# Weights fetched through ScalarE's queue, the keys' sums in another pool, and the second layer's cached keys turned during the first layer's projections

## The chip, the core and the metric

The kernel runs on one NeuronCore of a Trainium2 chip. The metric is device time in microseconds of one execution of the program; times are compared as medians of several executions. In the profile, PE is TensorE (matrix multiplication), PEld its weight loads, ACT is ScalarE, DVE is VectorE, POOL is GpSimd, and SP is the engine that issues most DMAs. An engine's DMA-issuing instructions carry a q behind the engine's name (SPq, ACTq).

## What is computed

A two-layer encoder step on 2048 prompt frames and 64 sample frames, model width 1024, 16 heads of 64, all in fp32. Layer A is attention within a band of chunks with softmax, layer B a stick-breaking attention over all earlier frames:

```python
def reference(x_prompt, x_sample, cache_a_k, cache_a_v, cache_b_k, cache_b_v, norm_a, w_in_a, ...):
    qp, kp, vp, gp = a_project(xp, norm_a[i], w_in_a[i])       # RMSNorm, then one 1024 x 4096 projection
    op = chunk_band_prompt(qp, kp, vp, rel_bias_a[i])          # own chunk and 8 before it, softmax
    o_s = band_attend(qs, cache_a ++ ks, cache_a ++ vs, ...)
    xp = xp + gated_out(op, gp, w_out_a[i])                    # (o * silu(gate)) @ w_out
    kb_p, vb_p = shared_kv(xp, norm_kv, w_kv)                  # keys and values of layer B
    qp, gp = b_project(xp, norm_b[j], w_in_b[j])
    op = sb_prompt(qp, kb_p, vb_p)                             # w = exp(log_sigmoid(z) + sum of later log_sigmoid(-z))
    o_s = sb_block(qs, cache_b ++ kb_s, cache_b ++ vb_s, ...)
    xp = xp + gated_out(op, gp, w_out_b[j])
    y_prompt = rms_norm(xp, norm_f)
```

The outputs are the normed streams and the new rows of both key/value caches. Layer B's cache has 2048 rows, so its keys have to be brought into the layout [channel, row] once: this is the work that the change moves.

## The kernel before

Every fp32 product is split: an operand x is held as a high part (rounded to the format fp32r) and a low part, and hi·hi + hi·lo + lo·hi are added up in PSUM. Nothing fits into SBUF at once, so queries, keys, values, gates and outputs go through DRAM scratch tensors (`lay[L]`), as high and low parts.

The program has four stretches, two for each layer:

1. **Projections** (`projections`): first the values (tiles `ps_v`), then 24 jobs (three kinds by 8 head pairs, tiles `ps_t`): load a weight block (`wraw`, by ACT's queue), scale and split it, multiply, split the result, store it. Half of some kinds is left for later (`DEFER`): keys in layer A, queries and gates in layer B. Beside each job `stages.pop(0)` runs a share of a list of other preparations: `stage_cache` (load cached keys `kr`, turn them on PE as four 128x128 transposes `ps_c`, split, store), `stage_bias`, `stage_diff` (differences of values, on POOL), `stage_w_out` (split layer B's output weights and store them as `wo`). Before the change layer A's list has 56 entries, of which the last 8 are layer B's cached keys (8 of 32), and layer B's list has 74, of which 24 are the other cached keys.
2. **Attention**: items of four score tiles each (`z`), their weighting, transposes (`wt`), the split on ACT and DVE (`ph`, `pl`) and the products with the values (`acc`). An object `Beat` writes one item's parts out in beats, and beside them runs the steps of a second list, `beat.beside`: first the jobs left for later (`late_job`, products `ps_j`, weights `lwh` and `lwl`), then the output weights into two 4 MB tiles (`w_out_steps`, tiles `big`), then the output projection (`out_tile`, products `ps_o`). `Beat.step` takes one step at a time; each entry of the list has loads that run `ahead`, products, and work `behind`. The load of the next entry is started at the first product of the entry before.

What sets the order: the tile scheduler orders the instructions of each engine, except that within the attention the instructions that go through the wrapped engines (`InOrder`; `act`, `dve`, `gps`, `pe`, and `sp` for queue loads) keep the order in which the program is written. Each queue issues its DMAs in order, and a DMA waits at the head of its queue until its semaphores allow it. The semaphores of DMAs are eight (DMAHW0 to 7, handed out over all queues): a DMA also waits until the one before it on its semaphore has landed.

Names that the prediction uses: `vt`, `kt`, `q` are values, keys and queries loaded for the attention; `lkn` (in `add_back`) is the sum of a late key block's high and low part, made on POOL for the output rows; `sg` is a gate tile, stored as `gate_a` at the end of a projection job; `og`, `xr` are loads of the output projection. Tiles of a later stretch lie in memory that tiles of an earlier stretch have left, and then wait for their last readers, stores among them. All instructions that go through the wrapped engines show line L90 of the kernel (the wrapper); loads by the attention's `Queue` show L134, its stores L127.

Of the kernel before, what the change touches and what calls it, by code (L numbers as in the profile page):

```python
# [21 lines left out]
NP = 2048  # L22
# [28 lines left out]
STEP = 2  # L51

# [48 lines left out]
def encoder_step(ctx: ExitStack, tc: tile.TileContext, a: dict, o: dict):  # L101
# [634 lines left out]
    def late_job(L, kind, w, c0, g, hp, x2, first, prompt, rows_pool):  # L736
        st = {}

        def load():
            if L not in KEPT:  # L740
                st["raw"] = opool.tile([P, NK, P], F32, name="lraw", tag="og", bufs=1)
                c = c0 + hp * P
                sp.dma_start(st["raw"], w[:, c : c + P].rearrange("(k p) c -> p k c", p=P))
            st["wh"] = opool.tile([P, NK, P], F32R, name="lwh", tag="oh", bufs=2)
            st["wl"] = opool.tile([P, NK, P], F32R, name="lwl", tag="ol", bufs=2)
            if L in KEPT:
                for i, part in enumerate((st["wh"], st["wl"])):
                    sp.dma_start(f32(part), f32(lay[L]["w"][kind, hp][i]))
# [56 lines left out]
    def w_out_steps(src, w):  # L805
# [3 lines left out]
        def parts(k):  # L809
            if k == 0:  # L810
                w.extend(big_pair())
            for i in range(2):
                sp.dma_start(f32(w[i][:, k]), f32(wod[k][:, i]))
# [86 lines left out]
    class Beat:  # L900
# [4 lines left out]
        def __init__(self, lag, hold, scores_first, blank):  # L905
# [5 lines left out]
            self.now, self.at, self.ready, self.started = None, 0, 0, False  # L911
# [12 lines left out]
        def step(self):  # L924


            if self.now is None:
                self.now, self.at = self.beside.pop(0), 0
                ahead = self.now[0]
                if ahead and not self.started:  # L930

                    ahead.pop(0)()
                    self.ready = self.clock + 9
                self.started = False
# [16 lines left out]
            if self.at == 0 and following:  # L951
                rest.append(following.pop(0))
                self.started = True
# [7 lines left out]
            if self.at > half or n == 1:  # L961
                m = -(-len(following) // (n - self.at + 1))
                rest += [following.pop(0) for _ in range(m)]
# [100 lines left out]
    staged += keys_b[:8]  # L1064
    staged_b = []
    for i, (t, half) in enumerate((t, half) for t in range(len(TOK)) for half in range(2)):
        staged_b += [partial(stage_diff, "new", t, half), *keys_b[8 + i : 9 + i]]
# [19 lines left out]
    with (  # L1087
# [11 lines left out]
        beat.beside = job_steps("a", jobs_a, x2, NP - CACHE_A, o["a_k_p"], lpool)  # L1099
# [164 lines left out]
    with (  # L1264
# [45 lines left out]
        beat.beside = job_steps("b", jobs_b, x2, 0, o["b_k_p"], lpool)  # L1310
# [238 lines left out]
```

## Time and profile before

| | |
|---|---|
| median of three runs | 3279.95 us (3270.53, 3279.95, 3283.12) |
| profiled execution | 3271.0 us, its span 3269.2 us |
| granted TensorE clock, mean of the span | 0.996 |
| busy: PE, DVE, ACT, POOL | 98%, 58%, 52%, 40% |
| layer A: values, jobs, attention | 0 to 213, 213 to 668, 668 to 1312 us |
| layer B: values, jobs, attention and end | 1312 to 1624, 1624 to 2014, 2014 to 3269 us |

The page of the profile gives busy times of the engines, the span in 40 slices, the DMA queues, the chain of work that ended last, and the costliest groups of instructions. Busy time of PE is a modelled one: matmuls overlap, so 98% doesn't say that PE runs at its peak, but idle time of PE is real. Beside the page the trace is asked for the busy time of each engine and the granted clock in chosen stretches, for who waited for whom, for the chain in order of time, and for the instructions of one engine in order of time.

### The profile page before, as it was taken

What the parts mean: (1) busy time and instruction counts of PE and PEld (TensorE: products, weight loads), DVE (VectorE), ACT (ScalarE), POOL (GpSimd) and SP (SyncE); (2) the same over time, 40 slices, a digit from 0 to 9 for tenths busy, and PEclk for the clock granted to TensorE, in tenths of its full rate; (3) what the DMA queues carried; (4) which work ended last, traced back from release to release, by engine and by line L of the source; (5) the groups of instructions that cost most, each with busy time, mean ns of one, the idle gap of its engine ahead of it and who ended that gap; (6) DMA issues with size and microseconds to landing.
All of it is one profiled execution on the core that took longest, in us unless ns stands there. A gap on an engine that the chain in (4) does not pass through costs nothing.

```text
span 3269.2 us, 53693 instructions
## 1 busy us (share of the span) xinstructions
PE 3198.9 (98%) x17928; PEld 2786.8 (85%) x17928; DVE 1882.2 (58%) x3786; ACT 1709.0 (52%) x3719; POOL 1291.7 (40%) x1950
## 2 busy tenths in 40 slices
PE   8999999999998999999999999999999989999999
PEld 7889999988887898878899999888888878888877
DVE  4235431147778776232044432888878878888873
ACT  5234222258888776143143442666666656666662
POOL 3001110025655554020044200444477767777761
PEclk9999999999999999999999999999999999999999
DMA  6359993387899983453399999977735575355423
GB/s 202 122 185 373 347 331 119 118 241 218 239 261 267 252 231 121 168 183 132 107 352 347 351 352 341 274 218 215 210 121 151 160 208 174 119 144 143 136 72 120
DMA packets 464891, 688.41 MB, mean 211 GB/s; under 512 B 51445, under 2 KB 261397, under 8 KB 464614
## 3 DMA queue, kind: packets, MB, share of 16 engines
q1 hardware_dynamic: 405158, 633.85, 62.1%
q10 hardware_dynamic: 59456, 51.13, 4.8%
q8 instruction: 143, 2.34, 0.3%
q14 instruction: 134, 1.10, 0.1%
HBM read 408.78 MB, written 276.07 MB: 209 GB/s over the span
## 4 chain that ended last, share of the span: by engine, by line
PE 77%; issue 7%; DVE 7%; DMA 4%; ACT 3%; POOL 2%; SPq 0%; POOLq 0%; ACTq 0%; DVEq 0%
PE ps_t L90 24%; PE ps_v L90 11%; PE acc L90 10%; PE z L90 9%; PE wt L90 9%; PE ps_j L90 7%; PE ps_o L90 5%; DVE s L90 3%; DVE pl L90 2%; PE ps_tr L90 1%; ACT ph L90 1%; DMA keys<-k_a 1%; ACT s L90 1%; DMA vt<-v_b 1%; PE ps_c L90 1%
## 5 line engine op out<-in xcount | busy, mean ns | idle before, releaser
L90 DVE TENSOR_TENSOR pl<-wt,ph 128x512 fp32r<-128x512 f32 (+1 forms) x864 | 552.4, 654 | 121.8 <-ACT ph L90 117.9
L90 ACT ACTIVATE ph<-wt 128x512 fp32r<-128x512 f32 (+1 forms) x864 | 485.5, 577 | 203.4 <-PE wt L90 181.9
L90 PE MATMUL ps_t<-x_own,wh 128*128 128x362 f32 (+1 forms) x2304 | 568.1, 327 | 0.0
L90 PE MATMUL wt<-ident,s 128*128 128x128 f32 x3472 | 550.6, 274 | 14.7 <-DVE pl L90 6.9
L90 PEld LDWEIGHTS wt<-ident,s 128*128 128x128 f32 x3472 | 417.2, 141 | 90.3 <-DVE pl L90 13.1
L90 ACT ACTIVATE f<-z 128x512 f32<-128x512 f32 (+4 forms) x680 | 355.0, 536 | 189.4 <-PE z L90 131.8
L90 PEld LDWEIGHTS ps_t<-x_own,wh 128*128 128x128 f32 x2304 | 405.4, 188 | 1.8
L90 POOL TENSOR_TENSOR s<-f,s 128x256 f32<-128x256 f32 x416 | 360.1, 867 | 104.0 <-DVE s L90 96.7
L90 PE MATMUL acc<-ph,vt 128*128 128x512 f32 (+3 forms) x1088 | 374.6, 379 | 17.8 <-ACT ot L90 8.6
L90 PE MATMUL z<-kt,q 128*128 128x512 f32 (+3 forms) x1280 | 373.6, 379 | 4.2 <-ACT f L90 2.7
L90 PE MATMUL ps_t<-x_own,wl 128*128 128x362 f32 (+1 forms) x1152 | 377.2, 328 | 0.0
L90 PE MATMUL acc<-pl,vt 128*128 128x512 f32 (+3 forms) x1088 | 363.3, 367 | 7.4 <-DVE pl L90 7.1
L90 POOL TENSOR_SCALAR s<-s,rc 128x640 f32<-128x640 f32 (+5 forms) x264 | 199.3, 759 | 387.8 <-DMA keys<-k_a 194.1
L90 PE MATMUL ps_o<-big,oh 128*128 128x512 f32 x1088 | 336.3, 393 | 0.0
L90 POOL TENSOR_TENSOR two<-f 128x256 f32<-128x256 f32 x416 | 258.7, 624 | 155.1 <-ACT f L90 139.8
L90 DVE TENSOR_TENSOR_SCAN s<-two,s,own 128x256 f32<-128x256 f32 x408 | 300.2, 739 | 34.2 <-POOL two L90 32.8
L90 PEld LDWEIGHTS z<-kt,q 128*128 128x128 f32 x1280 | 220.2, 190 | 33.8 <-ACT f L90 9.3
L90 PE MATMUL ps_j<-big,lwh 128*128 128x512 f32 x768 | 246.8, 397 | 1.5 <-DVE pl L90 0.6
L90 PE MATMUL ps_t<-big,wh 128*128 128x512 f32 x768 | 239.1, 392 | 0.0
L90 PEld LDWEIGHTS ps_o<-big,oh 128*128 128x128 f32 x1088 | 202.3, 188 | 40.9 <-ACT oh L90 0.2
L90 PEld LDWEIGHTS acc<-ph,vt 128*128 128x128 f32 x1088 | 197.4, 190 | 41.1 <-ACT ot L90 11.2
L90 DVE CUSTOM_DVE_ANT_0 s<-z,bias 128x640 f32<-128x640 f32 (+4 forms) x256 | 184.8, 733 | 78.5 <-PE wt L90 52.8
(148 smaller groups left out, 5526.7 us busy)
## 6 DMA issues: line engine op xcount, KB each, us to landing
vt<-v_b SPq DMA_DIRECT2D x80, 512.0 KB, 4.5
v_b<-vs SPq DMA_DIRECT2D x64, 512.0 KB, 5.9
q<-q_a SPq DMA_DIRECT2D x128, 256.0 KB, 5.9
q<-q_b SPq DMA_DIRECT2D x128, 256.0 KB, 4.3
vt<-v_a SPq DMA_DIRECT2D x48, 512.0 KB, 7.9
kt<-k_b SPq DMA_DIRECT2D x96, 256.0 KB, 5.6
keys<-k_a SPq DMA_DIRECT2D x80, 256.0 KB, 6.8
v_a<-vs ACTq DMA_DIRECT2D x32, 512.0 KB, 2.7
```

Source lines behind the costliest of these rows:

```text
L90: ins = op(*args, **kwargs)
```

## The change

Five edits:

- The cached keys of layer B (`keys_b`) are all put on layer A's list (80 entries beside 24 jobs, where there were 56), and none stays on layer B's (50, where there were 74).
- `late_job` in layer B and `parts` in `w_out_steps` issue their weight loads from ACT's queue, where SP's issued them: 32 loads `lwh`, `lwl` and 16 loads `big`, 512 KB each.
- `Beat.step` starts the next entry's load two products later (`BEHIND`) where the entry has nothing but a load; and at entries without products it looks up to three entries ahead for the next load to start, so the first output tile's `og` and `xr` are loaded some steps earlier.
- `self.started` becomes `self.fetched`, which remembers whose load was started.
- The rows' tile `lkn` moves from the pools `band_l` and `sb_l` to `band_r` and `sb_r`.

```diff
+BEHIND = 2
...
                 for i, part in enumerate((st["wh"], st["wl"])):
-                    sp.dma_start(f32(part), f32(lay[L]["w"][kind, hp][i]))
+                    act.dma_start(f32(part), f32(lay[L]["w"][kind, hp][i]))
...
             for i in range(2):
-                sp.dma_start(f32(w[i][:, k]), f32(wod[k][:, i]))
+                act.dma_start(f32(w[i][:, k]), f32(wod[k][:, i]))
...
-                if ahead and not self.started:
+                if ahead and self.fetched is not ahead:
                     ahead.pop(0)()
                     self.ready = self.clock + 9
-                self.started = False
...
-            if self.at == 0 and following:
-                rest.append(following.pop(0))
-                self.started = True
+            coming = following
+            if n == 1:
+                coming = next((x[0] for x in self.beside[:3] if x[1] != [None]), [])
+            late = False
+            if coming and self.fetched is not coming and self.at == (BEHIND if n > 1 and len(coming) == 1 else 0):
+                rest.append(coming.pop(0))
+                self.fetched = coming
+                late = n == 1 and coming is following
+                if late:
+                    self.ready = self.clock + 9
...
-            if self.at > half or n == 1:
+            if self.at > half or n == 1 and not late:
...
-    staged += keys_b[:8]
+    staged += keys_b
     staged_b = []
-    for i, (t, half) in enumerate((t, half) for t in range(len(TOK)) for half in range(2)):
-        staged_b += [partial(stage_diff, "new", t, half), *keys_b[8 + i : 9 + i]]
+    staged_b += [partial(stage_diff, "new", t, half) for t in range(len(TOK)) for half in range(2)]
...
-        beat.beside = job_steps("a", jobs_a, x2, NP - CACHE_A, o["a_k_p"], lpool)
+        beat.beside = job_steps("a", jobs_a, x2, NP - CACHE_A, o["a_k_p"], rpool)
...
-        beat.beside = job_steps("b", jobs_b, x2, 0, o["b_k_p"], lpool)
+        beat.beside = job_steps("b", jobs_b, x2, 0, o["b_k_p"], rpool)
```

No arithmetic is added or removed: each engine has the same instructions as before, in another order, and 48 DMAs have another queue. Three places show the order. (Line numbers after the change are one higher: L91 for L90, L135 for L134, L128 for L127.)

The first is POOL at the start of layer A's attention, with what each instruction waits for; `vprev` ends the projections' differences, `s<-s,rc` is the softmax's scaling, `lkn<-sp` the first sum of keys. Before:

```order
L90 TENSOR_TENSOR vprev<-vprev,vcur 128x512 [waits DMAHW7_49,DMAHW1_49,DVE_49]
L90 TENSOR_TENSOR vprev<-vprev,vcur 128x512 [waits DMAHW4_49,DMAHW2_49,DVE_49]
L90 TENSOR_SCALAR s<-s,rc 128x640 [waits DMAHW3_49,DMAHW2_49,DMAHW4_49,DMAHW1_49,DMAHW5_49,DMAHW0_49,DMAHW6_49,DVE_49,DMAHW7_49,PE_49,Pool_49]
L90 TENSOR_SCALAR s<-s,rc 128x640 [waits DVE_49]
L90 TENSOR_TENSOR lkn<-sp 128x512 [waits DMAHW5_49,DMAHW1_49,DMAHW6_49,DMAHW0_49,DVE_49]
L90 TENSOR_SCALAR s<-s,rc 128x640 [waits DVE_49] x6
```

And after the change:

```order
L91 TENSOR_TENSOR vprev<-vprev,vcur 128x512 [waits DMAHW6_49,DMAHW4_49,DVE_49]
L91 TENSOR_TENSOR vprev<-vprev,vcur 128x512 [waits DMAHW2_49,DMAHW0_49,DVE_49]
L91 TENSOR_SCALAR s<-s,rc 128x640 [waits DMAHW3_49,DMAHW2_49,DMAHW4_49,DMAHW1_49,DMAHW5_49,DMAHW0_49,DMAHW6_49,DVE_49,DMAHW7_49,PE_49,Pool_49]
L91 TENSOR_SCALAR s<-s,rc 128x640 [waits DVE_49]
L91 TENSOR_TENSOR lkn<-sp 128x512 [waits DVE_49]
L91 TENSOR_SCALAR s<-s,rc 128x640 [waits DVE_49] x6
```

The sum stands at the same place in POOL's order; its waits for four DMA semaphores (stores of gate tiles `sg`, in whose memory it lay) are gone, and it waits for DVE alone.

The second is SP's queue in layer B's attention, where the output weights come in (`big_30644` and `big_30645` are their high and low halves). Before:

```order
L134 DMA kt<-k_b_122 64x2x512
L134 DMA vt<-v_b 128x4x256
L134 DMA kt<-k_b_122 64x2x512
L90 DMA big_30645<-wo_163 128x1024
L90 DMA big_30644<-wo_164 128x1024
L90 DMA big_30645<-wo_164 128x1024
L90 DMA big_30644<-wo_165 128x1024
L90 DMA big_30645<-wo_165 128x1024
L90 DMA og<-o_b_137 128x8x128
L90 DMA xr<-x_158 128x1024
L134 DMA vt<-v_b 128x4x256
L90 DMA big_30644<-wo_166 128x1024
```

The same keys and values after the change:

```order
L91 DMA xr<-x_158 128x1024
L128 DMA q_b_118<-sp 128x512 x3
L135 DMA kt<-k_b_122 64x2x512 x4
L135 DMA q<-q_b_114 64x2x512
L135 DMA kt<-k_b_122 64x2x512
L135 DMA vt<-v_b 128x4x256
L135 DMA kt<-k_b_122 64x2x512
L135 DMA q<-q_b_114 64x2x512
L135 DMA kt<-k_b_122 128x2x512
L135 DMA qs_21394<-q_b_116 64x2x64 x2
L135 DMA vt<-v_b 128x4x256 x5
L128 DMA o_b_138<-ot 128x512
```

Nothing but small stores stands between one `vt` and the next now; before, the second `vt` stood behind five `big` and the two loads of an output tile, which has moved ahead.

The third is ACT at the same place of the program, with its waits; `otmp<-total` ends a sample item. Before:

```order
L90 ACTIVATE ph<-wt 128x512 [waits DVE_49,PE_49] x2
L90 ACTIVATE f<-z 128x512 [waits PE_49,Pool_49]
L90 ACTIVATE ph<-wt 128x256 [waits DVE_49,PE_49]
L90 ACTIVATE otmp<-total_21401 64x64 [waits DVE_49] x2
L90 ACTIVATE f<-z 128x512 [waits PE_49,Pool_49]
L90 ACTIVATE ph<-wt 128x512 [waits PE_49] x2
L90 ACTIVATE f<-z 128x512 [waits Pool_49]
L90 ACTIVATE ph<-wt 128x512 [waits PE_49]
```

And after the change:

```order
L91 DMA big_30644<-wo_160 128x1024 [waits DMAHW7_49]
L91 DMA big_30645<-wo_160 128x1024 [waits DMAHW0_49]
L91 ACTIVATE f<-z 128x512 [waits PE_49,Pool_49]
L91 DMA big_30644<-wo_161 128x1024 [waits DMAHW1_49]
L91 DMA big_30645<-wo_161 128x1024 [waits DMAHW2_49]
L91 ACTIVATE ph<-wt 128x512 [waits PE_49] x3
L91 ACTIVATE f<-z 128x512 [waits Pool_49]
L91 ACTIVATE f<-z 128x512 [waits PE_49,Pool_49]
L91 ACTIVATE ph<-wt 128x512 [waits PE_49]
L91 ACTIVATE f<-z 128x512 [waits PE_49,Pool_49]
L91 ACTIVATE f<-z 128x512 [waits PE_49,Activation_49,Pool_49]
L91 DMA big_30644<-wo_162 128x1024 [waits DMAHW7_49]
```

ACT has taken over the 16 loads in eight pairs, one to eleven of its own instructions apart (in order 11, 1, 8, 7, 7, 7, 7), and each of them waits for the transfer before it on its semaphore.

More of the change, by code (lines that the diff above doesn't have):

```diff
@@ L910, in __init__ @@
             self.beside, self.rate, self.due = [], 0.0, 0.0
-            self.now, self.at, self.ready, self.started = None, 0, 0, False
+            self.now, self.at, self.ready, self.fetched = None, 0, 0, None
             self.steps, self.waiting = 0, []
```

## Prediction

> **What bounds the kernel now.** First the page: the span, PE's busy time, and the chain of work that ended last, by engine.
>
> ```profile
> span 3269.2 us, 53693 instructions
> PE 3198.9 (98%) x17928; PEld 2786.8 (85%) x17928; DVE 1882.2 (58%) x3786; ACT 1709.0 (52%) x3719; POOL 1291.7 (40%) x1950
> ...
> PE 77%; issue 7%; DVE 7%; DMA 4%; ACT 3%; POOL 2%; SPq 0%; POOLq 0%; ACTq 0%; DVEq 0%
> ```
>
> PE idles 3269.2 − 3198.9 = 70.3 us in all, and no product is removed. The change can win no more than idle time of PE and time at a low clock, and only at the places it touches. So next the windows of such places (from:to, length, busy time and instructions of PE, PEld, DVE, ACT, POOL, then granted clock, DMA share, GB/s):
>
> ```profile
> 213.00:668.00 455.00, 454.82 (x2524) 425.44 (x2523) 151.18 (x390) 142.44 (x370) 46.87 (x43) 1.00 0.72 255
> 668.00:706.00 38.00, 33.59 (x157) 28.52 (x156) 11.35 (x33) 12.19 (x28) 5.96 (x7) 0.96 1.01 281
> 700.00:706.00 6.00, 4.36 (x17) 4.03 (x18) 2.21 (x6) 1.10 (x3) 3.94 (x5) 0.72 0.84 215
> 1624.00:2014.00 390.00, 389.45 (x2294) 371.47 (x2293) 154.42 (x317) 154.67 (x384) 92.01 (x74) 1.00 0.97 349
> 2014.00:2046.00 32.00, 29.60 (x140) 24.47 (x139) 5.66 (x13) 5.80 (x11) 0.82 (x2) 0.95 1.00 307
> 2030.00:2040.00 10.00, 8.32 (x37) 6.27 (x36) 0.69 (x1) 0.60 (x1) 0.00 (x0) 0.83 1.08 288
> 2046.00:2600.00 554.00, 546.54 (x3196) 461.23 (x3196) 461.81 (x756) 360.19 (x742) 315.96 (x571) 1.00 0.68 195
> 2660.00:2700.00 40.00, 30.71 (x181) 25.73 (x180) 29.11 (x49) 22.19 (x47) 24.43 (x47) 0.91 1.06 326
> 2680.00:2690.00 10.00, 5.62 (x23) 4.99 (x24) 4.25 (x8) 3.45 (x7) 4.63 (x10) 0.66 1.06 317
> ```
>
> PE is full in the jobs of both layers (rows 1 and 4). It idles 38 − 33.59 = 4.4 us where layer A's attention starts (668 to 706), 2.4 us where B's starts (2014 to 2046), and 9.3 us of 40 where the output weights come in (2660 to 2700). Each time the clock falls too. Who was waited for there, by the waits (engine, tile, releaser: total us, times, longest):
>
> ```profile
> PE wt L90 <- POOL s L90: 4.4, 1, 4.4
> POOL lkn L90 <- DMA k_a<-sp: 6.0, 1, 6.0
> ...
> PE ps_j L90 <- DMA lwl<-w_bq: 1.2, 1, 1.2
> PE ps_c L90 <- DMA kr<-in_cache_b_k: 0.7, 1, 0.7
> PE ps_j L90 <- DMA lwh<-w_bq: 0.5, 1, 0.5
> ...
> PE acc L90 <- DMA vt<-v_b: 8.1, 2, 5.4
> ```
>
> **The keys' sum, layer A.** The chain in order of time (start, duration, what), and SP's row for a gate's store:
>
> ```profile
> 678.73 11.08 DMA keys<-k_a
> ...
> 689.87 9.67 DMA k_a<-sp
> ...
> 699.55 1.26 POOL lkn L90
> ...
> 688.77 0.33 SPq L408 DMA_DIRECT2D gate_a<-sg  x1
> ```
>
> POOL's first `lkn` starts at 699.55, when a store has landed; behind it on POOL stands the scaling `s` that PE's `wt` waits for. After the change this sum waits for DVE alone, and POOL goes on 6.0 us earlier, more than PE's 4.4 us of idling. With the low clock behind it (700 to 706 at 0.72, so 6 × 0.28 = 1.7 us) the term is −4.4 − 1.7 = **−6.1 us**. What is late next: ACT's `ph`, whose memory also waits for a gate's store (a rival below). The same move in layer B has no PE wait to remove.
>
> **B's late weights.** At 2014 to 2046 PE waits 0.5 + 1.2 us for `lwh` and `lwl` and 0.7 us for a cached key block `kr`; the clock is 0.83 over ten microseconds, 1.7 us. After the change B's cached keys are turned elsewhere, and these loads don't stand behind other transfers of SP: −2.4 − 1.7 = **−4.1 us**. Further on there is nothing to win: over 2046 to 2600 PE idles 7.5 us of 554. That later loads are started two products later I count as 0, since a load starts a whole job ahead of its use; at most it loses the time of two products, an estimate of 0.6 us from the two matmuls of 0.58 us quoted below.
>
> [...]
>
> **The output weights.** SP's queue (start, duration, instruction, count) and the issues (count, size, median us to landing):
>
> ```profile
> 2662.94 6.01 SPq L90 DMA_DIRECT2D big<-wo  x5
> 2669.65 0.37 SPq L90 DMA_DIRECT2D og<-o_b  x1
> 2671.96 3.44 SPq L90 DMA_DIRECT2D xr<-x  x1
> 2675.50 1.82 SPq L134 DMA_DIRECT2D vt<-v_b  x1
> ...
> 2684.41 0.38 SPq L134 DMA_DIRECT2D vt<-v_b  x1
> ```
>
> ```profile
> big<-wo SPq DMA_DIRECT2D x16, 512.0 KB, 9.0
> vt<-v_b SPq DMA_DIRECT2D x80, 512.0 KB, 4.5
> kr<-in_cache_b_k SPq DMA_DIRECT2D x32, 256.0 KB, 4.2
> vcur<-in_cache_b_v SPq DMA_DIRECT2D x32, 256.0 KB, 6.6
> ```
>
> Two `vt` are issued only at 2675.50 and 2684.41, behind five `big`, `og` and `xr`, and PE waits 8.1 us for them. After the change only small stores stand between the `vt`, so they are issued some 12 us earlier (2675.50 − 2662.94). I take away the 8.1 us and the low clock of 2680 to 2690 (10 × 0.34 = 3.4 us): **−11.5 us**. `og` and `xr`, loaded some steps earlier in both layers, I count as 0 (bounds −2 to +3, an estimate from the 3.44 us of `xr`).
>
> What it adds: 16 `big` on ACT, in eight pairs 11, 1, 8, 7, 7, 7, 7 of its instructions apart. Each waits for the transfer before it on its semaphore, and behind it on ACT stand `ph` and `f`, for which DVE's `pl` and PE's `wt`, `acc` and `z` wait. ACT runs 742 instructions in the 554 us from 2046 on, one per 0.75 us, so seven take 5.2 us, where a `big` landed after 9.0 us: a pair comes up to 3.8 us too early. Bounds: 0, if a `big` lands as fast as a `vt` (4.5 us), and 8 × 3.8 = 30 us. I take **+5**, near the lower end, since PE has work queued in `late` products and the transfers get the room that SP's burst took.
>
> The issue itself, in two rows of ACT (start, duration, what):
>
> ```profile
> 1651.94 0.64 ACT L90 ACTIVATE vs<-vprev 128x512 fp32r<-128x512 f32 x1 [0.70 <-POOL vprev L90]
> 1652.25 0.37 ACTq L379 DMA_DIRECT2D wraw<-in_w_kv  x1
> ```
>
> An issue takes 0.37 us and overlaps the ACTIVATE before it. 32 loads `lwh` and `lwl` come in 16 pairs, 0.75 us each, so 0 to 12 us; ACT is busy 360 of 554 us there and has slack between: **+2**.
>
> **The cached keys.** 24 groups of four transposes leave B's jobs and come into A's. The price on PE, from its rows and the group of the lines view for B's jobs:
>
> ```profile
> 582.98 0.60 PE L90 MATMUL ps_c<-ident,kr 128*128 128x128 f32 x4
> 583.34 0.58 PE L90 MATMUL ps_t<-x_own,wh 128*128 128x364 f32 x2
> ...
> L90 PE MATMUL ps_c<-ident,kr 128*128 128x128 f32 x96 | 14.4, 273 | 0.7 <-DMA kr<-in_cache_b_k 0.7
> ```
>
> A group holds PE from 582.98 to 583.34, 0.36 us: 24 × 0.36 = 8.6 us less in B and 8.6 us more in A, net **0**. The 24 loads of 256 KB go into A's jobs at a DMA share of 0.72. In B, at a share of 0.97, all 24 cost 0.7 us of waiting, so beside 0.72 I take 0; the upper bound is 24 × (6.6 − 4.2) = 58 us, if every `kr` came as late as a `vcur` does and nothing hid it. Below nothing it can't go by more than B's idle time: PE idles 0.55 us of 390 in B's jobs, so easing the DMA there buys nothing.
>
> **The sum.** −6.1 − 4.1 − 11.5 + 5 + 2 + 0 = −14.7 us. The profiled execution took 3271.0 us; 3256.3 after. The median of the runs, 3279.95, is 8.95 above it, so the median after is **3265.3 us**, −0.45%. A measurement of this kernel can tell about 0.5%, 16.4 us, from no change: the border is 3263.5, just under the forecast.
>
> **Rivals.** *The transfers bound the place, not the queue.* From 2660 to 2700 the DMA share is 1.06 at 326 GB/s, the most it shows beside B's jobs; the same bytes through another queue would land no earlier, and `vt` would share with ACT's `big`. Then the −11.5 goes and ACT's costs stay: −6.1 − 4.1 + 5 + 2 = −3.2, so 3267.8 profiled and 3276.7 as median. Against it: `vt` waited to be issued, not only to land. Chance 0.14. [...]
>
> *The change doesn't do what it says at A's start.* `ph` waits for stores of the same gates, issued at 688.77 beside the `k_a` store that landed at 699.54. If ACT is held as long as POOL was, the 6.1 stays: −8.6, so 3262.4 and as median 3271.4. Chance 0.12.
>
> *Slower: ACT's queue stands.* SP could stand at a DMA without harm, ACT cannot. The nearest row for a held DMA is SP's, in layer B up to 2675:
>
> ```profile
> SPq L134 <- PE z L90: 115.6, 41, 12.7
> ```
>
> 115.6 / 41 = 2.8 us each. The gross gain is 21.7 us, so it decides from 21.7 / 2.8, about 8 of the 24 pairs finding their semaphore's transfer not landed. If 14 pairs do and the bulk costs its bound: 14 × 2.8 + 30 − 21.7 = +47, so 3318 and as median 3327. Against it: the weights are prefetched a job ahead, so the transfer on the same semaphore is mostly old. Chance 0.09.
>
> *Slower: late keys in A's jobs,* at the 58 us above or half of it: 3285 to 3323. Chance 0.05.
>
> **How the numbers follow.** The forecast has 0.60; since its value lies near the border, 0.36 of it is below 3263.5 and 0.24 within. The first two rivals lie within, 0.14 + 0.12; standing ACT is 0.07 slower and 0.02 within, late keys 0.05 slower. Faster 0.36, same 0.52, slower 0.12. The range goes down to the full 21.7 us without any cost, less the scatter of the runs (3279.95 − 3270.53 = 9.4): 3249. Up it holds both rivals within and the bulk's bound of 30 in place of 5: 3265 + 25 = 3290.
>
> **What would show it.** Right: no wait of POOL's `lkn` for a store, no PE idling around 700; no `ps_j` wait after 2014; no PE wait for `vt` where the output weights come in; `ps_c` waits in A's jobs under 2 us. Wrong: PE waits there for `pl` or `ph` with ACT standing at a `big`; `vt` landing later though issued earlier; a half clock in A's jobs; `ph` waiting for a gate's store. The prediction fails first if ACT stands longer at its pairs than 5 us in all, or if layer A's jobs grow by more than the 8.6 us of transposes.

## The result

| | before | after |
|---|---|---|
| median of 13 runs each, us | 3273.45 (3270.35 to 3283.12) | 3267.68 (3263.90 to 3270.44) |
| ratio, 95% interval | | 0.9977 (0.9969 to 0.9985) |
| profiled execution, us | 3271.0 | 3269.4 |

The change makes the kernel 0.23% faster, some 7.5 us (5 to 10 by the interval): no change by the prediction's bound of 0.5%. The ratio is not the quotient of the two medians, here and below: the medians differ by 5.8 us here, and in the experiments the two measures lie up to 3.5 us apart. The forecast was −14.7 us, the right side and twice the size or more. Where the other half went takes the rest of this document: several terms of the sum were wrong.

The page of the kernel after: as many instructions of each compute engine as before, and the same bound.

```profile
span 3267.6 us, 53606 instructions
...
PE 79%; issue 8%; DVE 7%; DMA 3%; ACT 3%; POOL 2%; ACTq 0%; SPq 0%; POOLq 0%; DVEq 0%
```

Then the windows of the three places (columns as in the prediction), with those to which the idle time has gone:

```profile
668.00:706.00 38.00, 38.00 (x198) 33.66 (x197) 8.62 (x22) 10.29 (x25) 0.00 (x0) 1.00 0.72 219
700.00:706.00 6.00, 6.00 (x30) 5.06 (x29) 0.69 (x1) 0.60 (x1) 0.00 (x0) 1.00 1.07 306
720.00:730.00 10.00, 5.98 (x36) 5.64 (x35) 4.97 (x18) 4.85 (x15) 3.48 (x6) 0.75 1.10 299
2030.00:2040.00 10.00, 10.00 (x50) 8.11 (x49) 0.69 (x1) 0.60 (x1) 0.00 (x0) 1.00 1.03 326
2040.00:2050.00 10.00, 6.89 (x26) 5.42 (x25) 2.27 (x4) 1.81 (x5) 0.19 (x1) 0.83 1.09 260
2660.00:2700.00 40.00, 37.43 (x235) 31.08 (x233) 35.85 (x60) 28.26 (x59) 30.65 (x59) 1.00 1.03 305
```

PE idles 2.6 us where the output weights come in, where it idled 9.3, and the clock stays at 1.00. Around 700 and 2030 it is full now, but layer A's attention begins some 18 us later here, and the idle time stands at 720 to 730 instead, with the clock at 0.75; in layer B it stands at 2040 to 2050, at 0.83. Fixed windows mislead where everything shifts. So the comparison goes by the same matmul in both traces: each stretch runs from one named product to another, and the table has what a stretch takes more or less than in the first profile of before. A's jobs reach from the first `ps_t` to the first `z`; A's start from there to the 145th `ps_j`; the rest of A to layer B's first `ps_v`; the values to the last `ps_v`; B's jobs to the last `ps_t`; B's start to the 577th `ps_j`; the middle to the 1765th `z`; the output weights to the 2605th `wt`; and the end to the last `ps_o`.

| profile | A's jobs | A's start | rest of A | B's jobs | B's start | middle | weights | end | sum |
|---|---|---|---|---|---|---|---|---|---|
| before, us | 474.9 | 91.7 | 638.5 | 397.7 | 126.8 | 525.9 | 100.2 | 490.7 | |
| after | +17.8 | +0.7 | 0.0 | −11.7 | −2.5 | +2.4 | −8.4 | −0.1 | −1.9 |
| after, second profile | +14.8 | +1.3 | +5.1 | −11.7 | +3.0 | +1.2 | −8.8 | +0.6 | +5.5 |
| before, second profile | −0.4 | +0.5 | −1.3 | 0.0 | +3.6 | −0.1 | +0.2 | +0.7 | +3.2 |
| sum's pool alone | +3.5 | −4.9 | −1.5 | +0.5 | +6.3 | +0.9 | 0.0 | 0.0 | +4.8 |
| keys alone | +15.6 | −0.3 | +0.4 | −11.7 | −3.8 | 0.0 | +2.2 | −0.1 | +2.3 |
| queue alone | 0.0 | +1.9 | −2.2 | +0.5 | +11.0 | −0.2 | −7.8 | +0.9 | +4.1 |
| keys back | −0.1 | −4.1 | +2.0 | +0.7 | +6.7 | +1.2 | −8.5 | +0.8 | −1.3 |
| `big` on SP | +15.1 | +0.1 | −0.6 | −11.5 | +2.8 | +2.0 | +1.3 | +0.5 | +9.7 |
| late weights on SP | +14.2 | +0.2 | +0.3 | −10.7 | −1.3 | 0.0 | −8.5 | 0.0 | −5.7 |
| keys back, late weights on SP | +0.4 | −4.7 | +1.0 | +0.9 | +4.5 | +0.8 | −7.6 | +1.0 | −3.5 |
| keys spread evenly | +52.1 | −4.0 | +1.5 | −11.7 | +2.3 | +2.6 | −8.5 | +0.1 | +34.5 |
| sum's pool and `big` on ACT only | +1.4 | −4.8 | +2.6 | +1.0 | +1.2 | 0.0 | −7.3 | +0.6 | −5.5 |
| 24 keys, paced | +8.0 | −5.6 | +2.6 | −8.9 | +0.5 | +0.5 | −6.9 | +0.7 | −9.2 |

(The values of layer B, 202.4 us, are the same in all.) A row is one execution. Four columns agree among executions of like kernels within some 2 us: A's start, B's jobs, the middle and the weights. The others vary by several microseconds from one execution to the next. So the columns tell where, and the medians of runs tell how much.

### The profile page after: what moved, and what is told of

It is laid out like the page before. It is cut to its first block, busy times and chain, and to the rows that moved or that the text cites. A ratio compares the mean times of both kernels' runs of the same rounds, so it can differ in the third digit from the quotient of the medians.

```text
span 3267.6 us, 53606 instructions
## 1 busy us (share of the span) xinstructions
PE 3200.5 (98%) x17928; PEld 2786.0 (85%) x17928; DVE 1889.2 (58%) x3786; ACT 1712.5 (52%) x3719; POOL 1289.7 (39%) x1950
## 4 chain that ended last, share of the span: by engine, by line
PE 79%; issue 8%; DVE 7%; DMA 3%; ACT 3%; POOL 2%; ACTq 0%; SPq 0%; POOLq 0%; DVEq 0%
PE ps_t L91 25%; PE ps_v L91 11%; PE acc L91 10%; PE z L91 9%; PE wt L91 8%; PE ps_j L91 7%; PE ps_o L91 5%; DVE s L91 3%; DVE pl L91 2%; ACT ph L91 1%; PE ps_tr L91 1%; ACT s L91 1%; POOL s L91 1%; PE ps_c L91 1%; PE ps_n L91 0%
## 5 line engine op out<-in xcount | busy, mean ns | idle before, releaser
L91 DVE TENSOR_TENSOR pl<-wt,ph 128x512 fp32r<-128x512 f32 (+1 forms) x864 | 550.6, 653 | 105.6 <-ACT ph L91 102.0
L91 ACT ACTIVATE ph<-wt 128x512 fp32r<-128x512 f32 (+1 forms) x864 | 484.4, 577 | 191.2 <-PE wt L91 177.7
L91 PE MATMUL ps_t<-x_own,wh 128*128 128x362 f32 (+1 forms) x2304 | 568.9, 328 | 0.5 <-DVE sl L91 0.5
L91 PE MATMUL wt<-ident,s 128*128 128x128 f32 x3472 | 550.0, 274 | 11.1 <-DVE pl L91 9.5
L91 PEld LDWEIGHTS wt<-ident,s 128*128 128x128 f32 x3472 | 416.8, 140 | 85.6 <-DVE pl L91 14.4
L91 ACT ACTIVATE f<-z 128x512 f32<-128x512 f32 (+4 forms) x680 | 355.4, 536 | 199.1 <-PE z L91 131.2
L91 PEld LDWEIGHTS ps_t<-x_own,wh 128*128 128x128 f32 x2304 | 406.6, 188 | 2.5 <-DVE sl L91 0.7
L91 POOL TENSOR_TENSOR s<-f,s 128x256 f32<-128x256 f32 x416 | 360.2, 867 | 104.1 <-DVE s L91 96.0
L91 PE MATMUL acc<-ph,vt 128*128 128x512 f32 (+3 forms) x1088 | 375.0, 379 | 10.0 <-ACT ot L91 8.2
L91 PE MATMUL ps_t<-x_own,wl 128*128 128x362 f32 (+1 forms) x1152 | 377.3, 328 | 0.0
L91 PE MATMUL z<-kt,q 128*128 128x512 f32 (+3 forms) x1280 | 372.4, 377 | 3.3 <-ACT f L91 3.0
L91 PE MATMUL acc<-pl,vt 128*128 128x512 f32 (+3 forms) x1088 | 363.7, 368 | 8.5 <-DVE pl L91 8.0
L91 POOL TENSOR_SCALAR s<-s,rc 128x640 f32<-128x640 f32 (+5 forms) x264 | 199.2, 759 | 391.7 <-DMA q<-q_a 190.5
L91 PE MATMUL ps_o<-big,oh 128*128 128x512 f32 x1088 | 336.1, 392 | 0.0
L91 POOL TENSOR_TENSOR two<-f 128x256 f32<-128x256 f32 x416 | 259.3, 625 | 154.5 <-ACT f L91 135.8
L91 DVE TENSOR_TENSOR_SCAN s<-two,s,own 128x256 f32<-128x256 f32 x408 | 299.7, 737 | 35.5 <-POOL two L91 34.1
L91 PE MATMUL ps_j<-big,lwh 128*128 128x512 f32 x768 | 246.5, 397 | 3.7 <-ACT ends L91 3.1
L91 PEld LDWEIGHTS z<-kt,q 128*128 128x128 f32 x1280 | 220.2, 190 | 31.6 <-ACT f L91 8.9
L91 PE MATMUL ps_t<-big,wh 128*128 128x512 f32 x768 | 241.4, 394 | 0.0
L91 PEld LDWEIGHTS ps_o<-big,oh 128*128 128x128 f32 x1088 | 202.4, 188 | 40.9 <-DVE pl L91 0.2
L91 PEld LDWEIGHTS acc<-pl,vt 128*128 128x128 f32 x1088 | 194.2, 190 | 42.8 <-DVE pl L91 27.3
L91 DVE CUSTOM_DVE_ANT_0 s<-z,bias 128x640 f32<-128x640 f32 (+4 forms) x256 | 184.6, 732 | 79.4 <-PE wt L91 54.0
```

The costliest lines, as they stand in the source:

```text
L91: ins = op(*args, **kwargs)
```

## The experiments

### One edit at a time

The first kernel has the sum's move alone:

```diff
-        beat.beside = job_steps("a", jobs_a, x2, NP - CACHE_A, o["a_k_p"], lpool)
+        beat.beside = job_steps("a", jobs_a, x2, NP - CACHE_A, o["a_k_p"], rpool)
...
-        beat.beside = job_steps("b", jobs_b, x2, 0, o["b_k_p"], lpool)
+        beat.beside = job_steps("b", jobs_b, x2, 0, o["b_k_p"], rpool)
```

> The kernel before with the keys' sum lkn in the other pool and nothing else. Theory: POOL's wait for a gate's store goes, and the next thing late, the load of q that cost 4.0 us after the whole change, is only late there because 24 more key blocks are loaded and stored just ahead of it; so alone the move gives PE's 4.4 us and the low clock back, -6 us (ratio 0.998), with no wait of PE for q around 700. Rival: the q load is late whatever the keys do; then PE waits some 4 us for q instead of 4.4 us for POOL, and the time is the same within 1 us (ratio 1.000).

Measured: 3270.34 us against 3275.81, ratio 0.998 (0.997 to 0.999); A's start −4.9 us, and no wait for q around 700. The theory holds. In layer B this execution lost 6.3 us to another load, which the waits name:

```profile
PE z L90 <- DMA q<-q_b: 4.9, 1, 4.9
```

The second has the keys' move alone:

```diff
-    staged += keys_b[:8]
+    staged += keys_b
...
-    for i, (t, half) in enumerate((t, half) for t in range(len(TOK)) for half in range(2)):
-        staged_b += [partial(stage_diff, "new", t, half), *keys_b[8 + i : 9 + i]]
+    staged_b += [partial(stage_diff, "new", t, half) for t in range(len(TOK)) for half in range(2)]
```

> The kernel before with all cached keys of layer B on layer A's list and nothing else. Theory: A's jobs grow by more than B's shrink, as in the trace after the change (+17.7 us against -11.6 us, by the times of the same matmuls), so +6 us (ratio 1.002), 5 us of it in the first third of A's jobs, where the list is taken faster and layer A's own cached keys are wanted earlier. Rival of the prediction: 24 groups of 0.36 us only change their place, A's jobs +8.6 us, B's -8.6 us, the time the same (ratio 1.000).

Measured: 3272.71 us, ratio 0.9987 (0.9978 to 0.9995). Here the theory fails on the time: alone the keys' move costs nothing, it wins 3 to 4 us. In its profile A's jobs do grow by more (15.6) than B's shrink (11.7), but B's start is 3.8 us shorter, and A's start is no longer, although the sum lies in its old pool: the wait for POOL is not there any more, and in its place stands

```profile
PE z L90 <- DMA q<-q_a: 3.6, 1, 3.6
```

So it is the keys' move that makes q late at A's start, and what the sum's move wins alone is not to be had beside all the keys. The fourteen profiles divide cleanly here: where PE waits for this q (five profiles), the attention's first load of q is issued 14.7 us ahead of the first `z`; in the other nine it is 19.8 to 20.3 us ahead, and none waits.

The third has the 48 loads on ACT's queue alone:

```diff
-                    sp.dma_start(f32(part), f32(lay[L]["w"][kind, hp][i]))
+                    act.dma_start(f32(part), f32(lay[L]["w"][kind, hp][i]))
...
-                sp.dma_start(f32(w[i][:, k]), f32(wod[k][:, i]))
+                act.dma_start(f32(w[i][:, k]), f32(wod[k][:, i]))
```

> The kernel before with the loads lwh, lwl and big issued by ACT and nothing else (no later loads, no earlier og and xr). Theory: PE's 8.1 us for vt go and ACT's stops give a part back, -8 us in the place of the output weights; at B's start ACT stands at its first lwh for a transfer of SP, some 13 us, and PE waits 3 us for it, as much as was won there; -8 us in all (ratio 0.9975). Rival: without the earlier og and xr and the later loads the vt still come late (og and xr stand between them on SP's queue), and less than half of it is won, -4 us or less (ratio 0.999).

Measured: 3273.12 us, ratio 0.999 (0.9981 to 0.9998). The time is the rival's, the reason isn't. The place of the output weights is 7.8 us shorter without any edit to the order of the loads, and no wait for vt is left. The gain is lost at B's start, +11.0 us, as the waits there show (PE, then ACT):

```profile
PE ps_j L90 <- DVE sg L90: 6.4, 1, 6.4
PE z L90 <- ACT f L90: 5.0, 2, 4.8
...
ACT sg L90 <- DMA q<-q_b: 16.6, 1, 16.6
ACT f L90 <- DMA vt<-v_b: 11.9, 1, 11.9
```

ACT stands twice, 16.6 and 11.9 us, each time with a pair `lwh`, `lwl` at the head of its program. What it waits for are loads by SP, a `q` and a `vt`.

### The changed kernel with one edit undone

The keys divided 8 and 24 again:

```diff
-    staged += keys_b
+    staged += keys_b[:8]
...
-    staged_b += [partial(stage_diff, "new", t, half) for t in range(len(TOK)) for half in range(2)]
+    for i, (t, half) in enumerate((t, half) for t in range(len(TOK)) for half in range(2)):
+        staged_b += [partial(stage_diff, "new", t, half), *keys_b[8 + i : 9 + i]]
```

> The changed kernel with the cached keys divided 8 and 24 again, as before the change. Theory: the keys cost 6 us by themselves and another 6 us by the late q at A's start, so the changed kernel without their move is 10 to 14 us faster than before (ratio 0.996 to 0.997), with no wait of PE for q around 700. Rival: the keys are free and q is late anyhow; then it stands where the changed kernel stands, -6 to -8 us (ratio 0.998).

Measured: 3266.23 us against 3275.81, ratio 0.996 (0.9946 to 0.9973), −13 us by the ratio and −10 by the medians: the theory's range. A's start is 4.1 us shorter, no wait for q. But the theory had this kernel only win, and it pays at B's start, +6.7 us. ACT's rows there (start, duration, what, idle before and its releaser):

```profile
2023.57 0.60 ACT L91 ACTIVATE sg<-ps_j 128x512 f32<-128x512 f32 x1 [3.59 <-PE ps_j L91]
2038.24 0.33 ACTq L91 DMA_DIRECT2D lwh<-w_bg  x1
2040.22 0.33 ACTq L91 DMA_DIRECT2D lwl<-w_bg  x1
2040.59 0.60 ACT L91 ACTIVATE sg<-ps_j 128x512 f32<-128x512 f32 x1 [16.43 <-DMA q<-q_b]
```

ACT issues this `lwh` of a gate job after 14.1 us without work and its `lwl` 2.0 us later. `sg`, queued behind both, comes after 16.4 us, and PE's products wait 6.3 us for DVE's part of `sg`.

Then `big` on SP again:

```diff
-                act.dma_start(f32(w[i][:, k]), f32(wod[k][:, i]))
+                sp.dma_start(f32(w[i][:, k]), f32(wod[k][:, i]))
```

> The changed kernel with the loads big issued by SP again (lwh and lwl stay on ACT). Theory: the queue bounded the place of the output weights, as the queue-alone kernel showed (no wait for vt left); with big back, PE waits some 8 us for vt again, and the 8 us that the change gained there are gone: about the time of before (ratio 1.000). Rival of the prediction: the transfers bound the place, or the earlier og and xr alone did it; then it stands where the changed kernel stands (ratio 0.998).

Measured: 3275.97 us against 3276.79, ratio 0.9999 (0.999 to 1.0008). The theory holds: without this edit nothing is left of what the change wins, and PE waits for vt as before:

```profile
PE acc L91 <- DMA vt<-v_b: 9.7, 2, 6.2
```

And `lwh` and `lwl` on SP again:

```diff
-                    act.dma_start(f32(part), f32(lay[L]["w"][kind, hp][i]))
+                    sp.dma_start(f32(part), f32(lay[L]["w"][kind, hp][i]))
```

> The changed kernel with lwh and lwl issued by SP again (big stays on ACT). Theory: ACT's stand of 13.8 us at its first lwh at the start of layer B's attention is what PE waits 3.1 us for there (ACT's ends); with the loads on SP it goes, -3 to -4 us against the changed kernel (ratio to before 0.9965). Rival: on SP they hold the loads of keys and queries behind them, and PE waits as long for lwl or q as it did for ends (ratio 0.998, as the changed kernel).

Measured: 3265.45 us, ratio 0.9971 (0.9961 to 0.9982) beside 0.9977 (0.9969 to 0.9985) for the change: not told apart. The wait for ends is gone, and the rival's wait is there in its place:

```profile
PE z L91 <- DMA q<-q_b: 3.0, 1, 3.0
```

The middle is 0.0 here, against +2.4 and +1.2 in the two profiles of the changed kernel. That is not the price of ACT's issues by themselves: the queue-alone kernel has the same 22 issues of `lwh` and `lwl` on ACT there, and its middle is −0.2. Only the kernels that have them together with the new order of the loads lose 1.2 to 2.6 us, at PE's waits for DVE's `pl` (the middle of the changed kernel, then of the queue alone):

```profile
PE wt L91 <- DVE pl L91: 2.6, 7, 0.7
...
PE wt L90 <- DVE pl L90: 1.2, 4, 0.7
```

The same edit and the keys' division together, by the two diffs above:

> The changed kernel with the cached keys divided 8 and 24 again and lwh and lwl issued by SP; what is left of the change is the sum's pool, big on ACT, and the order of the loads. Theory: with the keys back ACT stood 16.4 us at its first lwh and PE 6.3 us for it, and the clock fell; on SP that is 1.7 us of waits for lwh and lwl as before, so 5 to 8 us less than with the keys back alone, 15 to 20 us less than before (ratio 0.994 to 0.9955), the fastest of all. Rival: what was lost at ACT is lost at SP; then as with the keys back alone (ratio 0.996).

Measured: 3262.75 us, ratio 0.9965 (0.9952 to 0.9977), beside 0.996 with the keys back alone. The rival: B's start still loses 4.5 us, now to q (`PE z` waits 4.5 us for it) and not to ACT.

### Where the keys stand in A's jobs

The list of layer A with the 32 key blocks spread evenly through it:

```diff
-    staged += keys_b
+    own, staged, keys_b = staged, [], keys_b[:]
+    for i, x in enumerate(own):
+        staged.append(x)
+        while keys_b and (32 - len(keys_b)) * len(own) < 32 * (i + 1):
+            staged.append(keys_b.pop(0))
```

> The changed kernel with layer B's cached keys spread evenly through layer A's list, so that A's own cached keys and the differences keep the pace they had before. Theory: the 5 us that A's jobs lose in their first third (PE 2.1 us for kr of layer A's cache, and the products of the new keys) come from the list being taken four entries a job where it was three; spread evenly that goes, -5 us against the changed kernel (ratio 0.996), and the 12 us of the later two thirds move to the whole. Rival: this loss comes from the state of the transfers and not from the pace, since the kernel with the sum's move alone showed 4 us of it too; then the ratio is 0.998, as the changed kernel's.

Measured: 3300.58 us against 3276.79, ratio 1.0078 (1.0064 to 1.0092). Both expectations fall: this is 24 us slower than before. The waits, and the window in which they lie, of this kernel:

```profile
PE ps_c L91 <- DMA kr<-in_cache_b_k: 16.2, 3, 8.3
PE ps_c L91 <- DMA kr<-in_cache_a_k: 11.6, 2, 9.7
```

```profile
300.00:420.00 120.00, 89.63 (x463) 81.67 (x462) 46.74 (x116) 34.75 (x81) 24.94 (x22) 0.84 0.98 357
```

And three windows of A's jobs in the kernel before:

```profile
300.00:420.00 120.00, 120.00 (x655) 111.26 (x655) 49.72 (x125) 36.23 (x93) 21.09 (x17) 1.00 0.97 349
420.00:540.00 120.00, 120.00 (x636) 109.69 (x636) 35.38 (x76) 35.72 (x88) 17.03 (x13) 1.00 0.70 250
540.00:640.00 100.00, 100.00 (x544) 92.19 (x543) 15.09 (x42) 24.53 (x63) 0.00 (x0) 1.00 0.33 116
```

The prediction used 0.72 as the DMA share of A's jobs. That is a mean: from 300 to 420 the share is 0.97 already. With key blocks put there PE waits 27.8 us in five waits, four of them before 420, and runs at 0.84 of the clock, while from 420 on the share in the kernel before is 0.70 and 0.33. The late keys that the prediction held for unlikely are real where key blocks stand in the first half of these jobs. And A's start didn't wait for q in this kernel (−4.0 us), though key blocks stand on its list to the end: it seems to be their number there that decides.

So, the last question: 24 blocks in A, four a job in jobs 17 to 22, none in the last two jobs, with `lwh` and `lwl` on SP (the empty entries set the pace):

```diff
-    staged += keys_b
+    own, staged = staged, []
+    for i in range(0, len(own), 3):
+        staged += own[i : i + 3] + [lambda pool: None]
+    staged += keys_b[:24] + [lambda pool: None] * 8
...
+        staged_b += [partial(stage_diff, "new", t, half), *keys_b[24 + i : 25 + i]]
...
-                    act.dma_start(f32(part), f32(lay[L]["w"][kind, hp][i]))
+                    sp.dma_start(f32(part), f32(lay[L]["w"][kind, hp][i]))
```

> The changed kernel with lwh and lwl on SP, and 24 of the 32 cached key blocks on layer A's list, four a job in its jobs 17 to 22, behind three other entries a job in the first sixteen, and none in the last two; eight stay on layer B's. Theory: where the keys stand decides. In this stretch of A's jobs the DMA share was 0.33 to 0.70, so 16 blocks more cost about what they give back in B (8 us each way), no transfer of theirs stands before the attention's q, so the sum's 6 us are won, and B's start has less on its queue than with the keys back: -12 to -17 us against before (ratio 0.995 to 0.9965). Rival: any key block more in A's jobs makes q late at A's start; then the ratio is 0.997 to 0.998, as with all of them.

Measured: 3261.79 us against 3275.66, ratio 0.996 (0.9948 to 0.9972), −13 to −14 us: the theory. A's start is 5.6 us shorter; 16 more blocks cost A's jobs 8.0 us and give B's 8.9 back. SP's rows show why q is in time here. After the change:

```profile
687.72 0.32 SPq L237 DMA_DIRECT2D k_b<-kh  x1
688.45 0.32 SPq L237 DMA_DIRECT2D k_b<-kl  x1
690.57 1.31 SPq L135 DMA_DIRECT2D q<-q_a  x2
```

With the keys paced:

```profile
666.64 0.38 SPq L91 DMA_DIRECT2D lraw<-in_w_in_a  x1
675.21 0.66 SPq L135 DMA_DIRECT2D q<-q_a  x1
```

And in the kernel before:

```profile
667.36 0.66 SPq L134 DMA_DIRECT2D q<-q_a  x1
```

The first `z` starts at 705.3 after the change and at 695.4 here, so the attention's first load is issued 14.7 us ahead of it in the one, behind the stores of key blocks, and 20.2 us ahead in the other, as in the kernel before (667.36 against 687.6). The q that PE waits for is a later one, the eighth: it is issued 12.8 us behind the first `z` after the change and 8.9 us behind it with the keys paced.

### What is left of the change, and the same kernels again

The kernel before with the sum's pool and `big` on ACT, nothing else:

```diff
-                sp.dma_start(f32(w[i][:, k]), f32(wod[k][:, i]))
+                act.dma_start(f32(w[i][:, k]), f32(wod[k][:, i]))
...
-        beat.beside = job_steps("a", jobs_a, x2, NP - CACHE_A, o["a_k_p"], lpool)
+        beat.beside = job_steps("a", jobs_a, x2, NP - CACHE_A, o["a_k_p"], rpool)
...
-        beat.beside = job_steps("b", jobs_b, x2, 0, o["b_k_p"], lpool)
+        beat.beside = job_steps("b", jobs_b, x2, 0, o["b_k_p"], rpool)
```

> The kernel before with the sum's move and big on ACT, and nothing else: the keys divided 8 and 24, lwh and lwl on SP, and the loads in the old order, without the earlier og and xr and the later starts. Theory: the order of the loads is worth nothing, these two edits make the whole gain, and it stands with the kernel that has the new order beside them (ratio 0.9965, 0.995 to 0.998), with no wait for vt. Rival: og and xr between the vt on SP keep a part of the 8 us; then PE waits 2 to 4 us for vt and the ratio is 0.9975 to 0.998.

Measured: 3264.81 us against 3275.66, ratio 0.9962 (0.995 to 0.9974). The theory: two edits, three lines, are worth at least the whole change, and no wait for vt is left. The four kernels at 0.996 to 0.9965 can't be told apart from each other; against the change's 0.9977 their intervals still touch, so that they beat it is likely and not settled.

And the two kernels of the comparison once more, unchanged, for a second profile. The kernel before:

> The kernel before, unchanged, for a second profile. The runs of before spread over 12 us. Theory: its first profile, 3271.0 us, shows a good execution, and the spread sits at the starts of the two attentions and in the first third of A's jobs, where a load lands just before or just after it is wanted; in another execution PE waits some 5 us more at one of these places (at layer B's start for q, as with the sum's move alone) and the rest of the program agrees within 1 us. Rival: the spread is even, every stretch some tenths of a per cent longer.

Measured: 3273.84 us in one run, and 3.2 us more in the sum of the stretches, 3.6 of it at B's start, where `PE z` waited 3.4 us for a load of gates (`gs`) that the first profile has in time. As the theory had it, but at one place only; the jobs of A agree.

The changed kernel:

> The changed kernel, unchanged, for a second profile. Theory: what the comparison of the first two profiles says is in the order and not in one execution: A's jobs +12 to +18 us against before, B's jobs -11.6 us, PE waiting for q at layer A's start and not for POOL, for ACT's ends at layer B's start, none for vt; only the first third of A's jobs differs by up to 5 us. Rival: the wait for q at A's start is an accident of that execution; then the 6 us of the sum's move show here.

Measured: 3276.83 us in one run, above all thirteen runs of the changed kernel in the comparison; runs of the kernel before taken beside it have a median of 3275.66. A's jobs are +14.8 and B's −11.7, and PE's waits have the same names:

```profile
PE z L91 <- DMA q<-q_a: 4.0, 1, 4.0
PE ps_j L91 <- ACT ends L91: 2.9, 1, 2.9
```

There is none for vt. What differs lies in A's first third, in the rest of A (an output tile waited for, `acc` behind ACT's `ot`, 8.7 us at the longest) and at B's start.

## Why the forecast came out in its range, term by term

**The keys' sum, forecast −6.1, measured +0.7 and +1.3.** The mechanism was right and its value a little high: −4.0 to −5.6 in the six kernels that have the sum's move without q being late. The step that failed is "What is late next: ACT's `ph`". It was the load of q, and the keys' move made it late. The rows after the change (the chain in order of time, then the wait):

```profile
718.10 8.91 DMA q<-q_a
```

```profile
PE z L91 <- DMA q<-q_a: 4.0, 1, 4.0
```

The rival "the change doesn't do what it says at A's start" had the loss and not the cause. Two edits, each right alone, met at one place.

**B's late weights, forecast −4.1, measured −2.5 and +3.0.** The waits for `lwh`, `lwl` and `kr` went as forecast, but "these loads don't stand behind other transfers of SP" was wrong. On ACT's queue they wait for a semaphore that SP's transfers share, and then ACT stands. In the first profiles of before and after eight semaphores tell of the landings, of 250 or 251 DMAs each, 225 to 238 of them issued by SP and 12 to 26 by ACT. On the semaphores whose landings are all on record (999 pairs of successive DMAs before, 750 after) none is issued until the one before it has landed; the soonest starts 0.016 us behind. The `lwh` at 2044.44 has a `kt` before it, which SP issues at 2034.38, 3.4 us after ACT's last instruction has ended, and which lands at 2044.37 (ACT in order of time, and PE's wait):

```profile
2030.41 0.60 ACT L91 ACTIVATE sg<-ps_j 128x512 f32<-128x512 f32 x1 [3.48 <-PE ps_j L91]
2044.44 0.33 ACTq L91 DMA_DIRECT2D lwh<-w_bg  x1
2044.82 0.60 ACT L91 ACTIVATE sg<-ps_j 128x512 f32<-128x512 f32 x1 [13.81 <-DMA kt<-k_b]
2045.31 0.28 ACT L91 ACTIVATE ends<-ps_e 128x136 f32<-128x136 f32 x1
```

```profile
PE ps_j L91 <- ACT ends L91: 3.1, 1, 3.1
```

That is the rival of the standing queue, priced at 2.8 us a pair, with a stop of 13.8 us, of which 3.1 reach PE. In the second profile the same stop takes 13.6 us (2.9 for PE), and the next pair makes another, for which PE waits 3.2 us more:

```profile
2086.36 0.33 ACTq L91 DMA_DIRECT2D lwh<-w_bq  x1
2088.56 0.33 ACTq L91 DMA_DIRECT2D lwl<-w_bq  x1
2088.99 0.60 ACT L91 ACTIVATE ph<-wt 128x512 fp32r<-128x512 f32 x1 [5.35 <-DMA q<-q_b]
```

It decides at B's start, not at the output weights where the prediction looked for it: at the `big` pairs ACT's idle time before its next instruction is at most 1.56 us in the first profile. With the keys in B's jobs the first stop is 16.4 us and 6.3 for PE, so the keys' move takes back a part of what the queue costs there. Putting the loads back on SP wins nothing that the runs can tell (0.9971 beside 0.9977, and 0.9965 beside 0.996): then q is late, by 3.0 and 4.5 us. Only with the loads in their old order does SP look better, +1.2 beside +11.0 us at B's start, in one execution each.

**The output weights, forecast −11.5 + 5 = −6.5, measured −8.4 and −8.8.** The term that was right. If the 11.5 is right, its cost was set too high, some 3 us for 5. The `vt` that was issued at 2675.50, 4.9 us behind the 1765th `z` (2670.6), is the first of five now, 7.0 us ahead of it (2677.1), the 12 us that were forecast:

```profile
2670.14 11.57 SPq L135 DMA_DIRECT2D vt<-v_b  x5
```

The rival of the transfers is refuted: the bytes are the same (685.0 MB over SP's and ACT's queues), the DMA share is 1.03 where it was 1.06, the queue's edit alone wins 7.8 us there, and putting `big` back on SP takes the whole gain away (0.9999). What is saved lies in the order of the queue: a `vt` that stood behind five `big`, `og` and `xr` is issued 12 us earlier.

**ACT's issues, forecast +2, measured +2.4 and +1.2** in the middle. The number is right by luck. The issues alone cost nothing there (−0.2 with the queue alone); the loss needs the new order of the loads beside them, which the prediction put at 0. By which step this order makes `pl` late stays open.

**The cached keys, forecast 0.** From the 1153rd `ps_t` on the 24 blocks cost 12.4 us in every kernel that has them at the end of the list (+5.3 to +17.8 after the change), and B's jobs give 11.7 back in most: the net of 0.7 was about right, the price of a block was not (0.5 us, not the 0.36 that one group showed). What the term left out lies before. Between the 577th and the 768th `ps_t` the five profiles with all keys at the end of the list, which is taken four entries a job there, lose 1.8 to 1.9 us: PE waits 0.7 us before a `ps_n`, which turns new keys, and 0.5 us for `sl` behind it. Where the list's older entries are taken three a job, in the kernel before and seven other profiles, nothing is lost there. That and q at A's start are the price. The rest of the early loss is not the keys': before the 384th `ps_t` all profiles lie between −0.4 and +3.5 us, and the two longest, after the change (+3.4) and with the sum's move alone (+3.5), are those where PE waits 2.0 to 2.1 us for one `kr` of layer A's cache; after the change the clock is 0.50 for 3.41 us behind it (236.88 to 240.29).

**Later starts, earlier og and xr, forecast 0**: with the late weights on SP the kernels with and without them have 0.9965 and 0.9962. With the late weights on ACT they come with the loss in the middle told above.

**The signs.** Of the prediction's signs of being right one held whole, no wait for vt. The wait of `lkn` went, but PE idles 4.0 us twenty microseconds later; `ps_j` waits 3.1 us after 2014; `ps_c` waits 2.1 us in A's jobs in one profile and 0.7 in the other. Both ways in which it said it would fail first came: ACT stands longer than 5 us at a pair, and A's jobs grow by 17.8 and 14.8 us, more than 8.6. One of its sums is wrong, without weight for the rest: 3285 to 3323 for late keys mixes the profiled execution with the median; from 3265.3 it is 3294 to 3323.

Between the means of two profiles each, these terms make about −3 us (A's start +0.8, B's start −1.6, weights −8.7, middle +1.9, the jobs of A and B +4.8), and the runs say −7.5. The rest can't be placed: the two profiled executions of the change (3269.4 and 3276.8) lie in the upper part of its runs or above it, those of before (3271.0 and 3273.8) don't, and the stretches that vary between executions are those between the terms. It stays open what they are in a typical execution.

That the time after came out 2.4 us from the forecast (3267.68 for 3265.3) is luck. The median before was taken as 3279.95, from three runs; with thirteen it is 3273.45. So the start was 6.5 us too high and the gain 7 to 9 us too large, and the two errors cancel. The range of 41 us also holds the kernel before, unchanged.

## What to carry to other kernels

When a wait is taken away, ask for the next late thing in the order that the whole change makes, not in the old trace: the stall for POOL was replaced by a load that another edit of the same change had pushed back. Cover for moved transfers must be read from the stretch in which they land; a mean share of 0.72 was 0.97 and 0.33, and key blocks cost nothing net (8.0 − 8.9) or 40 us (52.1 − 11.7) by where they stood. For a load on a compute engine's queue, ask what its semaphore still waits for when the engine comes to it: on ACT it was cheap at the `big` (1.56 us of idle ACT at most), and dear at B's start, where ACT stood until transfers of SP had landed (stops of 13.6 to 16.6 us).

## What the runs showed of the hardware

The prediction read the clock as a mean over six or ten microseconds. In finer windows the records show how it fell. In the first profiles of the kernels before and after, the granted clock is 1.00 or 0.50 in every record. Leaving out the first 20 us and the last 8 us, it is 0.50 in four stretches of each: before from 702.53, 1016.56, 2033.73 and 2682.26, for 3.41, 6.83, 3.41 and 6.83 us; after from 236.88, 724.98, 1035.60 and 2045.94, for 3.41, 6.83, 6.83 and 3.41 us. The mean of 0.83 from 2030 to 2040 before is one such stretch, 1.7 us lost in 3.41 us at half. Four windows of 3.41 us at A's start, in the kernel before:

```profile
695.70:699.12 3.42, 1.54 (x12) 1.27 (x10) 2.65 (x11) 3.42 (x10) 0.00 (x0) 1.00 1.06 392
699.12:702.53 3.41, 0.89 (x5) 0.79 (x6) 0.00 (x0) 0.17 (x2) 2.98 (x4) 1.00 1.07 338
702.53:705.94 3.41, 3.41 (x14) 3.18 (x13) 2.15 (x6) 1.04 (x3) 1.41 (x2) 0.50 0.67 144
705.94:709.36 3.42, 3.42 (x25) 3.08 (x25) 2.81 (x10) 3.42 (x11) 1.16 (x2) 1.00 0.93 263
```

And after the change:

```profile
721.57:724.98 3.41, 1.56 (x12) 1.30 (x10) 2.50 (x9) 3.00 (x9) 1.02 (x3) 1.00 1.08 336
724.98:728.39 3.41, 1.24 (x5) 1.27 (x6) 0.54 (x4) 0.00 (x0) 0.00 (x1) 0.50 1.16 247
728.39:731.80 3.41, 3.41 (x17) 3.31 (x17) 1.25 (x4) 2.05 (x5) 1.65 (x3) 0.50 1.02 314
731.80:735.21 3.41, 3.41 (x24) 3.12 (x23) 2.00 (x6) 2.17 (x6) 1.76 (x2) 1.00 0.35 73
```

The stop of 4.4 us before lies in two of these windows, with 1.88 and 2.52 us of idle PE, and 3.41 us at half followed; the shorter one after the change, 4.0 us, lies in two with 1.85 and 2.17 us, and 6.83 us were at half. So here the length of the stop alone doesn't give the time at half. In the windows of 3.41 us just ahead of the eight falls PE idled 2.52, 2.28, 1.29 and 3.24 us before and 2.09, 1.85, 2.43 and 3.11 us after. The clock stayed at 1.00 behind windows with 1.88 us (695.70 to 699.12) and 1.55 us (931.20 to 934.60) before and with 1.41 us (2684.16 to 2687.57, where the output weights come in) after. A window with 1.29 us is among those ahead of a fall, at B's start before (2030.31 to 2033.73), and one with 1.88 us is not: what decides stays open. (The ends of matmuls are modelled, and so is this idle time.)
